# One decoder layer: four stages behind barriers replaced by one task graph ordered by a simulated list scheduler

## The chip, the cores and the metric

The kernel runs on all eight cores of one Trainium2 chip (two dies, cores 0 to 3 and 4 to 7). Each core takes one prompt sequence of 2048 rows and sixteen of the 128 sample rows, and nothing passes between cores. The metric is device microseconds of the slowest core. Names used below: TensorE (PE in the profile; PEld is its weight load), VectorE (DVE), ScalarE (ACT), GpSimd (POOL) and SyncE (SP, which here only issues DMAs).

Some executions of an eight-core program fall into a slow state, in which the cores of a die show a lower granted clock.

## The reference, cut to what matters

```python
def hybrid_layer(x, mem_k, mem_v, lru_h, lru_buf, sc_buf, ...):
    u = rmsnorm(x, norm_g)
    proj = u @ w_in                                   # (T,1024) @ (1024,8704)
    lx, lg, sb, scg, sh, sg, q, qg, mg = jnp.split(proj, SPLIT_POINTS, axis=-1)
    # branch A: conv(4) -> gated linear recurrence (width 768, 6 blocks of 128)
    xc, new_lru_buf = causal_dwconv(lx, lru_buf, lru_conv_w)
    xc = xc + lru_conv_b
    hs, new_h = rglru(xc, lru_h, ...)                 # two 128x128 gates per block, sqrt, exp, a scan over T
    z_a = (hs * jax.nn.silu(lg)) @ lru_wo
    # branch B: B * conv3(C * h)
    cy, new_sc_buf = causal_dwconv(scg * sh, sc_buf, sconv_w)
    z_b = (jax.nn.silu(sg) * sb * cy) @ sconv_wo
    # branch C: 4-head cross-attention into 256 memory tokens
    p = jax.nn.softmax(q·k / sqrt(128)); o = p·v
    z_c = (o * jax.nn.silu(qg)) @ xa_wo
    # merge, output projection, residual
    g_a, g_b, g_c = jnp.split(jax.nn.sigmoid(mg), N_BRANCH, axis=-1)
    y = (g_a * z_a + g_b * z_b + g_c * z_c) @ w_out
    return x + y, new_h, new_lru_buf, new_sc_buf      # a final rmsnorm follows outside
```

Prompt rows and sample rows share all weights. The samples have their own cached states, and their own cached keys and values (512 KB of each per sample row).

## The kernel before

It is written stage by stage: load and normalise x, keys and values; attention; branches A and B; merge; output. A barrier stands between the stages. After it, every engine listed waits until all other engines and DMAs have come as far as they had been written.

```python
    def barrier(self, skip=(), no_wait=()):
        targets = {}
        for k, st in self.streams.items():
            if st.cnt: targets[k] = st.cnt            # how far each engine has been written
        for k, v in self.dma_cnt.items():
            if v and k not in skip: targets[k] = v    # and each DMA queue
        # ... every stream not in no_wait then waits for all of them
```

The tokens are projected in two halves of 1024 (matmuls of 512 columns) and the samples apart, in matmuls of 16 columns:

```python
        HALVES = [(0, 1024), (1024, 2048)]
        def unit_half(lhs_list, rhs_arr, lo, reads):
            pp, tk = next_pp()                        # one of three PSUM tiles
            for b in range(2):
                pairs = [(lhs_list[k], rhs_arr[:, k, lo + b * 512: lo + (b + 1) * 512]) for k in range(nk)]
                mm_group(pp[:, b * 512:(b + 1) * 512], pairs, reads, tk, last_inc=(b == 1))
        def unit_samp(lhs_list, rhs_arr, reads):
            pairs = [(lhs_list[k], rhs_arr[:, k, T:TT]) for k in range(nk)]   # 16 columns
```

The order within a stage is written by hand, by stepping through generators (`adv("A", n)`, `adv("B", n - 1)`, ...).

The softmax here doesn't subtract the row's maximum and nothing guards it: scores larger than these inputs give would overflow.

## Time and profile before

| kernel before | value | where from |
|---|---|---|
| median time | 919.21 us (914.86 to 923.75, 3 runs) | the runs |
| core spans in the profiled run | 907.5 to 922.5 us | head of the page |
| TensorE busy | 782.2 us | busy table |
| next busiest engine | VectorE 427.6 us | busy table |
| 100 to 548 us (attention and branches) | TensorE busy 388 of 448 us | windows |

The prediction below quotes the lines. A busy share on the page is an average over stages: the merge stage is solid TensorE, the stages before and after are full of waits. So the windows say more than the busy table.

### The profile page before, as it was taken

The numbers are of one execution on the slowest core, as the hardware profiler recorded it, in microseconds if no ns is written. First come the engines' busy times: TensorE is split into PE (matmuls) and PEld (weight loads), VectorE is DVE, ScalarE is ACT, GpSimd is POOL, SyncE is SP. The second block draws the span as 40 slices with busy tenths as digits, with TensorE's granted clock in tenths as the row PEclk, the third lists the DMA queues.
The fourth block names the chain that finished last, engine by engine and source line by source line (L and its number), as shares of the span: only waits on it lengthen the run. The fifth ranks groups of instructions, "written<-read, shape, count | busy, mean of one in ns | idle before, by whom it ended". The sixth has DMA issues, their size and how long they took to land.

```text
span 922.5 us, 11753 instructions; the slowest of 8 cores (907.5 to 922.5 us)
## 1 busy us (share of the span) xinstructions
PE 782.2 (85%) x4199; PEld 360.4 (39%) x4199; DVE 427.6 (46%) x418; ACT 341.9 (37%) x423; POOL 238.6 (26%) x234
## 2 busy tenths in 40 slices
PE   0537799567999998999989659999999999999882
PEld 0434333123444444444444224444444444444331
DVE  0247322743244868585859692323223323323555
ACT  2414333655255564747382622111111111112332
POOL 2010056531120201112121214425435433222110
PEclk9967888678889999999999959999999999999996
DMA  8994156257470242524262307426336243003775
GB/s 174 212 223 76 47 118 158 91 77 106 42 68 1 25 45 24 46 23 47 24 58 23 35 8 69 43 26 69 30 40 69 23 47 36 12 1 97 247 239 175
DMA packets 107364, 68.58 MB, mean 74 GB/s; under 512 B 82595, under 2 KB 94965, under 8 KB 107291
## 3 DMA queue, kind: packets, MB, share of 16 engines
q0 software_dynamic: 96896, 39.26, 35.3%
q1 hardware_dynamic: 10411, 28.57, 9.7%
q8 instruction: 34, 0.56, 0.3%
q14 instruction: 23, 0.19, 0.1%
HBM read 88.96 MB, written 9.82 MB: 107 GB/s over the span
## 4 chain that ended last, share of the span: by engine, by line
PE 65%; DVE 10%; ACT 10%; DMA 8%; issue 5%; SPq 1%; POOL 0%; DVEq 0%; ACTq 0%; POOLq 0%
PE PP L365 61%; DMA R<-xp 8%; ACT R L978 2%; DVE R L962 2%; DVE R L999 1%; DVE R L1250 1%; PE PS L365 1%; ACT R L1259 1%; SPq L127 1%; DVE R L769 1%; ACT R L1056 1%; ACT R L767 1%; ACT R L768 1%; ACT R L986 1%; DVE og L771 1%
## 5 line engine op out<-in xcount | busy, mean ns | idle before, releaser
L365 PE MATMUL PP<-uT,wslot 128*128 128x512 bf16 x2176 | 511.3, 392 | 12.2 <-ACT R L1041 6.7
L365 PEld LDWEIGHTS PP<-uT,wslot 128*128 128x128 bf16 x2176 | 212.8, 100 | 277.8 <-issue 74.1
L365 PE MATMUL PP<-R 128*128 128x512 bf16 (+1 forms) x384 | 97.9, 396 | 37.3 <-DVE R L769 11.9
L1182 ACT ACTIVATE R<-PP 128x1024 f32<-128x1024 f32 x48 | 49.2, 1026 | 211.5 <-PE PP L365 206.2
L1191 DVE SCALAR_TENSOR_TENSOR R<-R,PP 128x1024 f32<-128x1024 f32 x32 | 39.1, 1221 | 152.0 <-PE PP L365 152.0
L127 POOL DMA_DIRECT2D wslot<-w_in x64 | 56.6, 904 | 52.0 <-PE PP L365 48.3
L365 PEld LDWEIGHTS PP<-R 128*128 128x128 bf16 (+1 forms) x384 | 33.6, 98 | 89.3 <-issue 57.8
L1195 POOL TENSOR_TENSOR R<-R 128x1024 f32<-128x1024 f32 x16 | 37.5, 2343 | 110.5 <-DVE R L1191 110.5
L1198 POOL TENSOR_TENSOR R<-R 128x1024 bf16<-128x1024 f32 x16 | 37.5, 2347 | 60.2 <-DVE R L1191 30.1
L810 POOL TENSOR_TENSOR R<-R 128x1024 f32<-128x1024 f32 x16 | 37.5, 2346 | 38.3 <-ACT R L809 25.0
L813 DVE TENSOR_REDUCE R<-R 128x8 f32<-128x1024 f32 x16 | 19.5, 1217 | 53.6 <-POOL R L810 53.6
L962 DVE SCALAR_TENSOR_TENSOR R<-R,pT 128x2048 f32<-128x2048 f32 x18 | 42.3, 2351 | 4.0 <-ACT R L958 2.4
L365 PE MATMUL PP<-gB,wslot 128*128 128x512 bf16 x192 | 44.1, 379 | 0.0
L365 PE MATMUL PP<-gA,wslot 128*128 128x512 bf16 x192 | 44.1, 379 | 0.0
L1187 DVE SCALAR_TENSOR_TENSOR R<-R,PP 128x1024 f32<-128x1024 f32 x16 | 19.5, 1221 | 52.4 <-PE PP L365 49.3
L1061 DVE SCALAR_TENSOR_TENSOR R<-R,pT 128x2048 f32<-128x2048 f32 x12 | 28.2, 2352 | 20.4 <-ACT R L1058 19.8
L1259 ACT ACTIVATE R<-R 128x1024 f32<-128x1024 f32 (+1 forms) x17 | 18.0, 1057 | 53.0 <-DVE stat L1274 41.1
L1250 DVE SCALAR_TENSOR_TENSOR R<-PP,R 128x1024 f32<-128x1024 f32 (+1 forms) x17 | 20.8, 1224 | 30.9 <-DMA R<-xp 21.3
L968 POOL COPY SO<-R 128x3 f32<-128x3 f32 x6 | 1.1, 187 | 129.8 <-DVE R L950 129.8
L994 DVE SCALAR_TENSOR_TENSOR R<-R 128x2064 f32<-128x2064 f32 x6 | 13.8, 2308 | 38.3 <-ACT R L993 38.3
L476 ACT ACTIVATE R<-R 128x1024 bf16<-128x1024 f32 (+1 forms) x19 | 20.1, 1058 | 29.4 <-DMA R<-xp 28.2
L365 PE MATMUL PP<-og,wslot 128*128 128x512 bf16 x128 | 30.2, 379 | 0.0
(177 smaller groups left out, 813.8 us busy)
## 6 DMA issues: line engine op xcount, KB each, us to landing
wslot<-w_in POOLq DMA_DIRECT2D x60, 256.0 KB, 8.0
R<-xp SPq DMA_DIRECT2D x16, 512.0 KB, 12.5
R<-ck SPq DMA_DIRECT2D x16, 512.0 KB, 3.6
R<-xp POOLq DMA_DIRECT2D x16, 512.0 KB, 5.6
y_p<-R SPq DMA_DIRECT2D x16, 512.0 KB, 3.1
R<-cv POOLq DMA_DIRECT2D x16, 256.0 KB, 5.3
wslot<-w_in POOLq DMA_DIRECT2D x4, 512.0 KB, 23.2
R<-w_out POOLq DMA_DIRECT2D x8, 256.0 KB, 11.5
```

The source lines that it names most:

```text
L127: eng.dma_start(out=out, in_=in_, **kw).then_inc(sems[semkey], 16)
L365: S.op("pe", lambda e, l=l, r=r, i=i: e.matmul(out_ap, l, r, start=(i == 0), stop=(i == n - 1)), reads=reads, writes=[wtok], inc=(last_inc ...
L476: S.op("act", lambda e, xb_=xb_, nr=nr, ti=ti: e.activation(out=junk[0:nr, :], in_=xb_[0:nr, :], func=AF.Square, accum_out=stat[0:nr, ti:t ...
L810: S.op("pool", lambda e, kb_=kb_, qb_=qb_: e.tensor_tensor(out=prod, in0=kb_, in1=qb_.unsqueeze(1).to_broadcast([128, 2, 512]), op=ALU.mul ...
L962: S.op("dve", lambda e, k=k, cw=cw: e.scalar_tensor_tensor(out=xc[:, 0:T], in0=lxp[:, k:k + T], scalar=cw(k), in1=xc[:, 0:T], op0=ALU.mult ...
L1061: S.op("dve", lambda e, k=k, sw=sw: e.scalar_tensor_tensor(out=cy[:, 0:T], in0=cinp[:, k:k + T], scalar=sw(k), in1=cy[:, 0:T], op0=ALU.mul ...
L1182: S.op("act", lambda e, pp=pp, th_=th_: e.activation(out=th_, in_=pp[:], func=AF.Tanh, scale=0.5), reads=[tk], writes=[tth])
L1191: S.op("dve", lambda e, th_=th_, zp=zp: e.scalar_tensor_tensor(out=th_, in0=th_, scalar=1.0, in1=zp, op0=ALU.add, op1=ALU.mult), reads=[tt ...
L1195: S.op("pool", lambda e, acc=acc, th_=th_: e.tensor_tensor(out=acc, in0=acc, in1=th_, op=ALU.add), reads=[tth, tacc_], writes=[tacc_])
L1198: S.op("pool", lambda e, acc=acc, th_=th_, j=j, lo=lo, hi=hi: e.tensor_tensor(out=mT[:, j, lo:hi], in0=acc, in1=th_, op=ALU.add), reads=[t ...
L1250: S.op("dve", lambda e, pp=pp, yr_=yr_, xr_=xr_, nr=nr: e.scalar_tensor_tensor(out=yr_[0:nr, :], in0=pp[0:nr, :], scalar=0.5, in1=xr_[0:nr ...
L1259: S.op("act", lambda e, xr_=xr_, yr_=yr_, nr=nr, col=col: e.activation(out=xr_[0:nr, :], in_=yr_[0:nr, :], func=AF.Square, accum_out=stat2 ...
```

## The change

Its intent is that nothing waits for a stage any more. Every operation becomes a task with an engine, an estimated duration, the tokens that it reads and writes (a token is the name under which a piece of data is ordered), and a priority. A list scheduler simulates the five instruction streams while the program is built. Each time, it takes a ready task of the best priority, allots ring buffers, and emits the instruction at the end of that engine's stream. The chip then runs each stream in exactly that order. 2048 + 16 rows are cut into three units of 688 with the samples inside, and the four query blocks come first, while x is still arriving. The sample products move from GpSimd to VectorE, x in the output stage gets ten buffers, and PSUM is four tiles for all.

```diff
+BLK = 344
+UW = 2 * BLK
+NU = 3
...
-        HALVES = [(0, 1024), (1024, 2048)]
...
+        def unit(lhs, nk, rhs, u, reads, prio, hold=()):
+            ps = Handle(PS)                                   # one of four PSUM tiles
+            def mm(k, b):
+                c = u * UW + b * BLK
+                return lambda e: e.matmul(ps.ap[:, b * 512:b * 512 + BLK], lhs(k), rhs[:, k, c:c + BLK], ...)
+            G.pe([mm(k, b) for k in range(nk) for b in range(2)], nk * 2 * 0.1465, reads, [ps.tok], prio, hold)
...
-        S.barrier(no_wait=("pe",))            # and the other barriers between stages
...
+    def dve(self, fn, n, reads, writes, prio, mode=1):
+        return self._add("dve", (n / mode + 170) / 960.0, [fn], reads, writes, prio)   # the planned duration
...
+                for r, t in lst:
+                    if r <= m + 0.4:                          # ready within 0.4 us of the earliest
+                        k = t.prio
+                        if t.tset is not None and curset is not None and not (t.tset & curset):
+                            k += 20.0                         # would need another ScalarE table
+                        if bk is None or k < bk[0]:
+                            bk = (k, r, t)
...
+        for hd in range(4):
+            step(heads_q, hd)                                 # queries first
+        step(branch_A_lg, 0)
+        step(branch_B_sg, 0)
+        step(branch_A_lx, 0)
+        kv(pos)
...
+        m_xr += [Mem(f"xr{4 + i}", m_gB.off + i * 4096, 1024, F32) for i in range(6)]
...
+            G.dma("sp", [(dst, lambda y_=y_, nr=nr: y_.ap[0:nr, :])], nr * 4096, [y_.tok], [t_dram[4]], P, None)
```

The scan is entered with its 2048 columns, so it is planned as (2048 + 170)/960 = 2.31 us. The last line, the store of a result tile, names one token, `t_dram[4]`, as written by all seventeen stores.

## The prediction

> **What bounds the kernel now.** I read the page's busy table first, then the slices, then a table of stretches for the slowest core, then the chain that ended last, and last some single groups. Busy time first:
>
> ```profile
> PE 782.2 (85%) x4199; PEld 360.4 (39%) x4199; DVE 427.6 (46%) x418; ACT 341.9 (37%) x423; POOL 238.6 (26%) x234
> ```
>
> TensorE is busy 85%, nothing else is above half. So the kernel is TensorE plus the times when TensorE waits or is slow. Where these lie the slices tell:
>
> ```profile
> PE   0537799567999998999989659999999999999882
> PEclk9967888678889999999999959999999999999996
> ```
>
> The barriers stand at about 100, 233, 548 and 836 us (the lines of the chain change there). Busy time of each engine between them (the last fields are granted clock, DMA share, GB/s):
>
> ```profile
> 0.00:100.00 100.00, 46.19 (x349) 32.40 (x349) 39.32 (x61) 35.94 (x71) 10.22 (x21) 0.84 0.78 158
> 100.00:233.00 133.00, 104.42 (x468) 41.04 (x468) 51.49 (x59) 59.23 (x84) 54.08 (x38) 0.77 0.53 103
> 233.00:548.00 315.00, 283.85 (x1510) 127.59 (x1511) 209.62 (x172) 168.24 (x158) 53.34 (x79) 0.94 0.36 34
> 548.00:836.00 288.00, 288.00 (x1607) 134.36 (x1605) 81.21 (x77) 52.69 (x58) 109.97 (x79) 0.99 0.36 38
> 836.00:922.50 86.50, 59.72 (x268) 24.99 (x266) 45.92 (x52) 25.81 (x52) 10.97 (x18) 0.92 0.60 202
> ```
>
> TensorE idles 53.8 us in the front (load and normalise x), 28.6 in attention, 31.1 in branches A and B, nothing in the merge stage, 26.8 in the output stage: 140 us in all. The merge stage is TensorE's own bound and shows its rate, one step of it in the chain being
>
> ```profile
> 586.29 34.55 PE PP L365 x160
> ```
>
> so a 512-column matmul costs 34.55/160 = 215.9 ns; the next step starts 35.54 us later, and the 0.99 us between them holds 40 matmuls of 16 sample columns, 25 ns each. In the last stage the chain is a load of x behind two buffers, one such pair every 9 us for two tiles:
>
> ```profile
> by line: DMA R<-xp 50.8%; DVE R L1250 12.8%; ACT R L1259 12.1%; issue 6.5%; DMA R<-xs 3.9%; ACT stat L1266 2.5%; DVE R L1217 2.4%; DVE R L1276 1.5%; ACTq L105 0.5%; DVEq L105 0.4%; DVE stat L1274 0.2%; POOLq L166 0.2%; POOLq L126 0.0%
> ```
>
> How much of the 782 busy us is slowness? Work at full rate: 512-column matmuls 2176 (projections) + 512 (merge outputs) + 96 (attention) + 48 (gates) + 272 (output) + 16 (sample queries) = 3120 x 0.2159 = 673.6; 128 of 256 columns, by half of that, 14; 608 of 16 columns x 0.025 = 15; transposes 19 x 0.9 = 17; the rest about 8. Sum **728 us**. So 922.5 = 728 of work + 140 idle + 54 of slow clock and start-up in the busy time.
>
> **What the Trainium skill says.** (1) "TensorE: Matmul & The Clock Gate", section on 56 against 53.3 ns: back-to-back warm matmuls start every N / 2.4 GHz + about 2.5 ns, never under about 25 ns. The trace agrees: 215.9 ns for 512, 25 ns for 16. So I use 344/2.4 + 2.5 = 145.8 ns for the new width, an estimate by that page.
> (2) Same page, "What's actually happening": the clock is halved after idle windows, and a peak-current limiter takes a die to 13/16 once three of its cores run dense matmuls. The trace agrees only in part: this core is at 0.81 from 113 to 270 us, and at 0.50 from 55 to 75, but the other cores mostly run at 1.00 from 200 us on, and the 288 us of fully dense merge stage are at 0.99 to 1.00 on all eight.
> (3) "SBUF — State Buffer", on the shared port pair: VectorE operations with two SBUF inputs and GpSimd lock each other out for a whole instruction. The trace agrees:
>
> ```profile
> L771 DVE TENSOR_TENSOR og<-R,og x16: 692/693/2345, 172.3 to 231.4; 128x512 bf16<-128x512 f32 x16
> ```
>
> Minimum and median are 0.69 us, the longest 2.35, which is GpSimd's sample product (2.346 us each) in the way.
>
> **The change part by part.**
> *Units of 688.* T + 16 rows = 2064 = 3 x 688, each two matmuls of 344. Matmuls of 344: 68 column blocks x 8 x 6 = 3264, gates 72, merge outputs 8 x 16 x 6 = 768: 4104 x 0.1458 = 598.4 us. Of 512: keys/values 32, attention 96, sample queries 16, output 272: 416 x 0.2159 = 89.8. Transposes 17, small ones (sample values as single columns, states) 7. Sum **712 us**, 16 less than before: six times 145.8 is 875 ns for a weight block against 4 x 215.9 + 25 = 889. The program has 4859 matmuls instead of 4199, so more weight loads, but one takes 98 ns and lies beside a matmul of 146.
> It also removes the small evacuations of samples on ScalarE and VectorE, off the path.
> *Front.* The loads of x and the weights saturate the DMA engines until 78 us now (share 1.0 and above from 25 to 75), and the first projections begin at 76.6. In the new order, a unit of 688 needs six tiles of x, about 22 us in, and the seven first blocks (queries, one A and one B block) hold 7 x 7.0 = 49 us of TensorE work with nothing but x and their weights. The two x and weight streams are still one bandwidth: 19 x-tiles of about 1.6 us (4 KB packets, some 0.17-0.2 us each over 16 engines) and twelve weight blocks of 1024 packets at 47 ns over 16 engines (that is what the merge stage shows: share 0.365 of 200 us, 24869 packets), 3.0 us each: 30 + 36, from 8 us on, so x is complete at 65 to 75 us. But it is now hidden under the queries. Idle: 22 us before the sixth tile, some hiccups after, less about 6 of transposes: **25 us**, instead of 54.
> *Attention, branches and samples without barriers.* TensorE: 37 remaining blocks x 7.0 = 259, gates 10.5, attention 21, keys/values 8, samples 7: about 305 us, against the 448 us from 100 to 548 now. Does another engine hold it? VectorE in that stretch, by the durations of the page: per branch block 5 convolution steps x 2.35, the scan 4.42, five full passes (three of 2.31, two gate products 2.30) about 11.5, the minimum 1.23, six PSUM units x 0.9 = 5.4, small 1: about 33, x 6 = 198; attention 32 x 0.69 = 22; sample products and sums, moved here from GpSimd, 16 x (1.24 + 1.22) = 39: **262 us**. ScalarE: about 33 per block with table loads of 1.28, plus 12 per head: 246. All below 305, but from the first sample product to the merge stage (128 us of VectorE by the order of its instructions) TensorE has only about 800 matmuls, 117 us, + 7. So VectorE is level or just ahead there, and I allow **18 us** of TensorE idle for the whole stretch, against 60.
> *Merge.* 8 x (40 x 6 x 0.1458 = 35.0) = 280, against 8 x 35.54. Evacuation stays far below it (VectorE 9 x 0.9 = 8 a step).
> *Output.* Ten x buffers instead of two, loads begun while the merge stage ends, and no barrier. TensorE needs 272 x 0.2159 = 58.7; 17 MB at the about 320 GB/s that the front touches are 53. So TensorE sets it, with a tail of the last tile (sum 1.2, square 1.25, root 0.7, scale 1.3, store 3): **8 us**, where 86.5 us stood for the stage.
> *Clock.* TensorE is now the bound everywhere, so slow stretches count in full: **10 us**, less than the 54 because the cold front and the gaps shrink, more than nothing because of the limiter.
> Sum: 712 + 25 + 18 + 8 + 10 = **773 us**.
>
> **The rivals.** (a) *VectorE becomes the bound between front and merge.* For: 262 of 305 us, the sample work moved onto it, and a graph whose order is fixed when it is built: if the real scan (4.42 us) is longer than planned, everything behind waits. Against: 86% still leaves room, and 22 us of PSUM reads have four buffers. It would cost 20 to 30 us more: 800. (b) *The limiter.* For: 0.81 during 157 us on two cores now; the slowest core counts. A stretch like this costs 157 x 0.19 = 30 us when TensorE is the bound: 790 to 800. Against: the dense merge stage runs at full clock. (c) *DMA in the front hides nothing*: if x is complete only at 80 us and the key and value weights, which take x's buffers, 15 us later, TensorE runs dry once: +15 us. (d) *It goes better*: the order fills the sample region too, 712 + 20 + 6 + 8 + 4 = 750.
>
> **Range and chances.** None of (a) to (c) takes back the 140 us; all three together give about 840, still 8% faster. So the sign is nearly sure; wrong only if the fixed order deadlocks into long waits on the chip. I say 773, 8 in 10 between 745 and 810; faster by over 2% 0.97, within 2% 0.02, slower 0.01.
>
> **What would show it right or wrong.** Right: TensorE busy some 92% or more of the span; slices at 9 from about the fourth on; the 344-column matmuls 146 ns apart in the merge stage; no idle gap over 5 us between 100 us and the output stage; the output stage near 60 us with TensorE in the chain instead of the x load; VectorE near 85% busy in the branches. Wrong: a VectorE line behind most of TensorE's waits before the merge stage (a), granted clock under 0.93 on most cores (b), TensorE idle behind weight or x loads between 40 and 100 us (c), or matmuls of 344 columns clearly over 146 ns apart because weight loads don't hide.

## More of the kernel before

The output stage has two x buffers, and it writes the sum of the next tile ahead of the scaling of this one:

```python
        S.barrier(no_wait=("pe",))
        xr = [carve(i * 4096, 1024, F32) for i in range(2)]
        ...
        for ti in range(len(ftiles)):
            if ti + 1 < len(ftiles):
                f_stageA(ti + 1)      # load x, 16 matmuls, y = 0.5*PSUM + x (VectorE)
            f_stageB1(ti)             # root of the mean square
            if ti + 1 < len(ftiles):
                f_stageA2(ti + 1)     # sum of squares (ScalarE)
            f_stageB(ti)              # y = y * r * g (VectorE), store
```

## The result, and the profile after

The four runs of the changed kernel took 860.31, 859.96, 882.14 and 966.19 us. The last two are slow (in the 966 us run the cores of die 0 were granted 0.80 to 0.83, in the other cores 4 and 5 had 0.93), so the fast time is 860.1. The kernel before took 918.0 beside it (914.86 to 923.75). The ratio of the two is **0.938** (95%: 0.933 to 0.943), so the kernel is faster, but by some 58 us instead of the 146 forecast, and outside the range of 745 to 810. Ratios here are the mean time of one kernel's fast runs over that of the other's in the same rounds, so they are not quite the ratio of the medians quoted.

Compare with the prediction's lines, of the page after (core 3, a fast run). First busy us and share by engine, then the slices for TensorE and its clock:

```profile
PE 742.9 (87%) x4859; PEld 460.8 (54%) x4859; DVE 386.3 (45%) x367; ACT 339.1 (40%) x398; POOL 251.2 (29%) x301
...
PE   0699989789888977979896699999999999999880
...
PEclk9999999889989989989998899999999999999996
```

TensorE starts at once, in the second slice, but between slices 8 and 23 it sits at 6 to 9 where solid nines were forecast, and the last slices look as they did before. The same in windows (window, its length, busy us of PE, PEld, DVE, ACT and POOL, granted clock, DMA share, GB/s), cut where the keys and values, the merge stage and the output stage begin:

```profile
0.00:100.00 100.00, 69.95 (x537) 48.11 (x538) 27.20 (x45) 39.01 (x63) 54.95 (x85) 0.98 0.91 159
100.00:487.00 387.00, 329.67 (x2104) 196.62 (x2102) 244.47 (x207) 225.82 (x229) 67.24 (x87) 0.93 0.45 63
487.00:771.00 284.00, 283.33 (x1955) 190.15 (x1952) 73.09 (x81) 54.73 (x72) 111.60 (x95) 1.00 0.36 39
771.00:858.40 87.40, 59.99 (x272) 25.87 (x272) 41.58 (x35) 19.53 (x34) 17.43 (x36) 0.91 0.57 197
```

Two windows are wrong: the second (387 us; the 305 us of work plus 18 had been forecast) and the last (87 us for 60 of TensorE). The merge stage is as forecast; in the chain of waits it is one piece:

```profile
523.00 247.35 PE PP L726 x1696
```

247.35/1696 = 145.84 ns for a matmul of 344 columns; the prediction had 145.8.

**A measure used below.** A busy TensorE may still be slow, so for each run the matmuls between the first key/value matmul and the first output matmul were added up at what they would take back to back, N/2400 + 0.0025 us each and never under 0.025; for 344 columns that is the rate of the merge stage. Their sum is 582.4 us (575.6 in run 4, and 589.6 in run 6, which does one query block less before that stretch). The rest of the stretch is called **lost**. It has two parts: time in which TensorE is idle, and busy time beyond that rate, which includes slow clock and whatever the rule prices too low. On cores 0, 3 and 5 the changed kernel lost 85, 88 and 87 us, 55, 58 and 57 of them idle, nearly all before 487 us. (The expectations below were written with a count that took the matmuls at the edges of its 30 us windows twice. It made the losses some 6 us too small: their 80 is 87 here, their 83 between 100 and 487 us is 86.)

Core 3, with each term of the prediction's sum:

| term | forecast | measured | how |
|---|---|---|---|
| TensorE work | 712 | 702 | at the rate above: 60.7 before the stretch, 582.4 in it, 58.7 after |
| idle in the front | 25 | 30 | up to the first key/value matmul at 101.3 |
| idle from there to the first output matmul | 18 | 58 | 670.0 less 611.7 busy |
| idle in the output stage | 8 | 27 | 87.1 less 60.0 busy |
| busy beyond the rate (slow clock) | 10 | 41 | 10.5 front, 29.3 middle, 1.3 output |
| sum | 773 | 858 | span 858.4 |

So 40 of the 85 missing us are idle time between the front and the output stage, 19 idle time of the output stage, 5 that of the front, and 31 busy time beyond the rate; the work is 10 less.

The kernel before, counted in the same way, has 720 us of work; core 1, the slowest, which was granted 0.81 for much of the time from 111 to 271 us, has 140 idle and 62 of busy time beyond the rate, and core 3, which was not, 146 and 44. So on core 3 the 51 us from 909.9 to 858.4 are 18 of work, 30 of idle time and 3 of slowness. Between front and merge stage the idle time hardly changed: 60 to 64 us before (100 to 548), 58 now. Most of the idle time that was won lies in the front (54 before, 30 now).

**The middle.** What TensorE waited for between 100 and 487 us (line waiting, line that released it: us in all, times, longest):

```profile
PE PP L1003 <- DMA R<-cv: 13.7, 2, 6.9
PE PP L726 <- ACT R L790: 7.7, 14, 1.4
PE PP L726 <- DVE R L943: 6.4, 6, 4.0
PE PP L726 <- ACT R L930: 5.8, 5, 2.4
PE PP L964 <- DVE R L832: 4.8, 1, 4.8
```

L790, L943, L930 and L832 empty PSUM: gate tanh, attention product, attention exp, and the product for branch B. Of TensorE's 57 idle us in this window, ScalarE lines ended 24, VectorE lines 19 and the cached values (cv) 14. Another 29 us are busy time beyond the rate; in seven stretches of 6.8 to 10.2 us (the first at 166.0) the granted clock was 0.50, and an estimated 18 of the 29 are due to that. No engine is the bound: VectorE is busy 244 of the 387 us, ScalarE 226. The timeline shows how TensorE can wait for a VectorE that has time (start, us, engine, line, operation; in brackets the idle time before and what ended it):

```profile
327.30 1.28 ACT L801 ACT_TABLE_LOAD   x1
328.60 2.02 ACT L801 ACTIVATE R<-R 128x2064 f32<-128x2064 f32 x1
...
330.72 2.31 DVE L803 TENSOR_TENSOR R<-R 128x2064 f32<-128x2064 f32 x1 [7.11 <-ACT R L801]
...
333.13 4.42 DVE L804 TENSOR_TENSOR_SCAN R<-R 128x2048 f32<-128x2048 f32 x1
337.47 0.15 DVE L808 TENSOR_TENSOR R<-R 128x16 f32<-128x16 f32 x1
337.72 2.31 DVE L810 TENSOR_TENSOR R<-R 128x2064 bf16<-128x2064 f32 x1
...
339.95 1.65 DVE L832 TENSOR_TENSOR R<-PP,R 128x688 f32<-128x688 f32 x2
...
340.96 0.58 PE L964 MATMUL PP<-R 16*128 16x512 bf16 x1 [4.76 <-DVE R L832]
```

VectorE first stands idle for 7.11 us, because the next instruction in its stream needs a square root (L801), and that stands in ScalarE's stream behind another long pass, four evacuations of PSUM and two table loads (from 321.24 on). Then it runs a product, the scan and another product, 9.2 us in a row. Behind these stand, in the same stream, the two evacuations L832. No PSUM tile is free meanwhile, and TensorE is dry for 4.76 us. The Trainium skill, "Perfetto Trace Analysis", section "Tensor Engine Instruction (MATMUL, LD_WEIGHTS)", says "ACT/DVE/GPSIMD are strict FIFO"; this stretch agrees: a short evacuation cannot pass a long pass written ahead of it.

**The output stage.** The chain of waits there (start, us, what):

```profile
770.40 4.79 DMA R<-xp
775.29 1.24 DVE R L1138
...
781.00 15.81 DMA y_p<-R
796.92 1.24 DVE R L1138
798.29 1.16 ACT R L1141 x2
...
801.86 1.23 DVE R L1138
803.23 1.16 ACT R L1141 x2
...
806.80 1.22 DVE R L1138
```

The first store of y, issued at 781.00, took 15.81 us to land (the median store takes 2.7). The issue queue of SyncE shows what was ahead of it:

```profile
770.40 9.73 SPq L131 DMA_DIRECT2D R<-xp  x12
781.00 0.34 SPq L131 DMA_DIRECT2D y_p<-R  x1
783.27 3.78 SPq L131 DMA_DIRECT2D R<-xp  x2
796.89 0.34 SPq L131 DMA_DIRECT2D y_p<-R  x1
```

Twelve loads of x of 512 KB each, and the second store not before 796.89, because all stores write one token and each waits until the one before has landed. With four y buffers VectorE then stood still. The loads came in one burst because the x buffers lie in memory of the attention and branch products (`m_og`, `m_gB`), which the merge stage still reads: the first load was issued at 770.40, not while the merge stage ends, as the prediction has it. After that the tiles come 4.94 us apart (801.86 to 806.80), although TensorE needs 16 x 0.2159 = 3.45 for one: sum (L1138), squares (L1141), root on GpSimd and scaling run one after the other, because the fixed order of VectorE has the scaling of a tile ahead of the sum of the next one.

### The profile page after: what moved, and what is told of

Same layout as the page of the kernel before. It is cut to its first block, busy times and chain, and to the rows that moved or that the text cites. A ratio compares the mean times of both kernels' runs of the same rounds, so it can differ in the third digit from the quotient of the medians.

```text
span 858.4 us, 13185 instructions; the slowest of 8 cores (848.3 to 858.4 us)
## 1 busy us (share of the span) xinstructions
PE 742.9 (87%) x4859; PEld 460.8 (54%) x4859; DVE 386.3 (45%) x367; ACT 339.1 (40%) x398; POOL 251.2 (29%) x301
## 4 chain that ended last, share of the span: by engine, by line
PE 64%; ACT 9%; DVE 9%; issue 9%; DMA 4%; POOL 3%; ACTq 1%; DVEq 0%; POOLq 0%; SPq 0%
PE PP L726 61%; DVE R L804 2%; ACT R L1141 2%; DMA y_p<-R 2%; DVE R L1138 2%; ACT R L790 2%; DVE R L777 1%; POOL R L621 1%; DMA R<-sconv_w 1%; DVE R L803 1%; ACT R L939 1%; DMA R<-cv 1%; PE PP L866 1%; DVE R L838 1%; POOL R L633 1%
## 5 line engine op out<-in xcount | busy, mean ns | idle before, releaser
L726 PE MATMUL PP<-R 128*128 128x344 bf16 x4104 | 632.0, 315 | 34.4 <-ACT R L790 7.7
L726 PEld LDWEIGHTS PP<-R 128*128 128x128 bf16 x4104 | 402.1, 99 | 256.9 <-issue 55.4
L1101 DVE SCALAR_TENSOR_TENSOR R<-R,PP 128x688 f32<-128x688 f32 x72 | 62.7, 871 | 202.8 <-PE PP L726 202.7
L131 POOL DMA_DIRECT2D R<-w_in x68 | 60.4, 889 | 307.0 <-PE PP L726 270.3
L1095 ACT ACTIVATE R<-PP 128x688 f32<-128x688 f32 x72 | 53.6, 744 | 218.4 <-PE PP L726 218.4
L1134 PE MATMUL PP<-R 128*128 128x512 bf16 (+1 forms) x272 | 60.0, 379 | 8.4 <-DVE R L1138 7.3
L1105 POOL TENSOR_TENSOR R<-R 128x688 f32<-128x688 f32 x24 | 39.3, 1639 | 45.6 <-DVE R L1101 44.1
L1141 ACT ACTIVATE R<-R 128x1024 f32<-128x1024 f32 (+1 forms) x17 | 18.0, 1056 | 65.9 <-DVE R L1138 65.7
L1108 POOL TENSOR_TENSOR R<-R 128x688 bf16<-128x688 f32 x24 | 38.7, 1637 | 16.9 <-DVE R L1101 16.9
L777 DVE SCALAR_TENSOR_TENSOR R<-R 128x2048 f32<-128x2048 f32 x18 | 42.2, 2347 | 2.7 <-ACT R L774 1.9
L1145 DVE SCALAR_TENSOR_TENSOR R<-R 128x1024 f32<-128x1024 f32 (+1 forms) x17 | 21.8, 1283 | 28.6 <-POOL R L621 27.2
L838 DVE SCALAR_TENSOR_TENSOR R<-R 128x2048 f32<-128x2048 f32 x12 | 28.2, 2348 | 8.8 <-ACT R L835 8.4
L790 ACT ACTIVATE R<-PP,R 128x688 f32<-128x688 f32 x36 | 28.1, 833 | 6.8 <-PE PP L726 6.7
L1138 DVE SCALAR_TENSOR_TENSOR R<-PP,R 128x1024 f32<-128x1024 f32 (+1 forms) x17 | 20.5, 1218 | 14.5 <-DMA y_p<-R 6.5
```

The source lines that it names most:

```text
L131: eng.dma_start(out=out, in_=in_).then_inc(sems[semkey], 16)
L726: return lambda e: e.matmul(ps.ap[:, b * 512:b * 512 + BLK], lhs(k), rhs[:, k, c:c + BLK], start=(k == 0), stop=(k == nk - 1))
L777: G.dve(lambda e, k=k: e.scalar_tensor_tensor(out=xc[:, 0:T], in0=lxp[:, k:k + T], scalar=cw(k), in1=xc[:, 0:T], op0=ALU.mult, op1=ALU.add ...
L790: G.act(lambda e, ps=ps, dst=dst, u=u, bcol=bcol: e.activation(out=cols(dst, u), in_=pv(ps), func=AF.Tanh, scale=0.5, bias=dv[:, bcol:bcol ...
L838: G.dve(lambda e, k=k: e.scalar_tensor_tensor(out=cy[:, 0:T], in0=cinp[:, k:k + T], scalar=sw(k), in1=cy[:, 0:T], op0=ALU.mult, op1=ALU.ad ...
L1095: G.act(lambda e, ps=pg[u], th_=th_: e.activation(out=b3(th_.ap), in_=pv(ps), func=AF.Tanh, scale=0.5), UW, [pg[u].tok], [th_.tok], Px - 2 ...
```

## The experiments

**Theories.** T1: between front and merge the time is lost by the *order* in which the planner put each stream; another order of the same instructions loses much less. Rival R1: VectorE's amount of work, or the scan planned at 2.31 instead of 4.42 us, is the cause (rival (a) of the prediction). Rival R2: the lost time belongs to work that no order can hide. T2: the output stage loses its time to the shared token of the stores. Rival R3: to VectorE's serial order alone.

**1. A token of its own for each store.**

```diff
-            G.dma("sp", [(dst, ...)], nr * 4096, [y_.tok], [t_dram[4]], P, None)
+            G.dma("sp", [(dst, ...)], nr * 4096, [y_.tok], [Tok(f"y{ti}")], P, None)
```

> Every store of y gets its own ordering token instead of one that all 17 share; nothing else changes in the source, and the plan changes only in the output stage. Theory A (the shared token makes each store wait until the one before has landed, the first of them landed 15.8 us after its issue behind twelve loads of x, and the plan built a serial order of VectorE around it): the output stage falls from 88 us to 62-70, the whole from 860 to 835-842, the ratio to the kernel before to about 0.915. Rival B (the output stage is held by DMA bandwidth, 17 MB): it stays above 80 us and the time within 5 us of 860.

Measured: 845.92 us (844.25 to 847.72), ratio 0.920 (0.916 to 0.923); still correct. The lost time of the middle stayed at 86 to 89 us, and the time is somewhat above the 835 to 842 expected. In the output stage the chain of the slowest core (core 2) is now TensorE itself:

```profile
772.92 64.35 PE PP L1134 x272
```

On core 3 the stage lasts from 770.4 to 843.5, 73 us instead of 87. The token alone accounts for some 14 us.

**2. The sum of the next tile ahead of the scaling of this one** (the order that the kernel before had), the token left shared.

```diff
+            if ti > 0:
+                G.after(tscale, tsum)      # scaling of tile ti-1 is placed after the sum of tile ti
```

> The shared token stays; only VectorE's order in the output stage is forced: the sum of tile t+1 always before the scaling of tile t. Instructions of TensorE are the same. If the serial chain sum, square, root, scale of 4.94 us a tile is the bound after the first stall (theory A, second half), the ten tiles from 797 us on go at 3.5 to 3.8 us instead of 4.94 and the time falls by 10 to 14 us, to about 848. If the landing of the stores is the bound instead, a tile still takes 4.5 us or more and the time falls by less than 5 us.

Measured: 847.04 us (844.15 to 915.9, one of them slow), ratio 0.920 (0.916 to 0.924), lost in the middle 86 to 87. The same gain as run 1 by the other way. But the chain is another one. TensorE doesn't set the stage here; the stores do, one behind another (core 3):

```profile
779.34 15.25 DMA y_p<-R
794.65 4.93 DMA y_p<-R
799.65 2.92 DMA y_p<-R
...
827.69 2.68 DMA y_p<-R
```

So neither T2 nor R3 is right as stated: the late store and the serial order are both needed for the 87 us. The first store is as late as before, but the tiles behind it now catch up at the pace of the stores, mostly 2.6 to 3.1 us each, instead of 4.94. Either remedy is enough to gain 13 to 14 us.

**3. The scan planned with its measured length.**

```diff
-                                                 op0=ALU.mult, op1=ALU.add), T, t_thr + t_thi, [t_xcP], P)
+                                                 op0=ALU.mult, op1=ALU.add), 4073, t_thr + t_thi, [t_xcP], P)
```

4073 stands for (4073 + 170)/960 = 4.42 us in the planner; the instruction is the same.

> The list scheduler is told the scan's true length (4.4 us instead of 2.3); the instructions are the same, only the order changes. Theory W (the fixed order is bad because VectorE's longest operation was planned at half its length): idle of TensorE between 100 and 487 us falls from 83 to 60 or less and the time by 15 us or more. Theory P (the order is already that sparse in the plan itself, wrong lengths are secondary): within 6 us of 860, to either side.

Measured: 850.73 us (849.10 to 909.13, one of them slow), ratio 0.924 (0.920 to 0.928). Lost 76 to 80 us, 7 to 9 less than before, which lies between the two theories. The wrong length is a cause, but a small one, and R1 in this form doesn't carry the loss.

**4. Without the samples' attention.**

```diff
-                sample_scores(pos, 5.0)
-                sample_values(pos + 90, 1.5)
+                pass
```

> Sample scores and sample values are left out (the sample rows of y are wrong on purpose). They are 7 us of TensorE work and 39 us of VectorE. If VectorE with the sample work on it holds the stretch before the merge stage and the waits for cached values (14 us) are real, the time falls by 25 to 38 us, to about 828, and the lost TensorE time between 100 us and the merge stage from 83 to 50-60. If the sample work hid in idle time anyway, it falls by no more than its own 7 us.

Measured: 819.73 us (819.51 to 820.09), ratio 0.891 (0.888 to 0.894). Lost 54 to 56 us, 31 to 32 less, beside some 7 us less of TensorE work; idle 37 to 38. The edit takes away more than 40 us of VectorE work (346.7 instead of 386.3 in the busy table): the loads of the cached keys and values go too, and the order changes. TensorE's waits for cached values (10 to 14 us) are gone, while the idle time that VectorE lines end falls only from 19 to 16. So this run doesn't show that VectorE's load holds TensorE.

**5. Without table switches** (Silu, Sqrt and Ln replaced by Tanh). The planner no longer sees switches, so the order changes too.

```diff
-EXP = frozenset((0, 6))
-SILU = frozenset((18,))
+EXP = None
+SILU = None
...
-            G.act(lambda e: e.activation(out=a2, in_=a2, func=AF.Sqrt, ...
+            G.act(lambda e: e.activation(out=a2, in_=a2, func=AF.Tanh, ...
```

> Silu, Sqrt and Ln are replaced by Tanh, so that all ScalarE functions share one table and no table is loaded between them (32 loads of 1.28 us in the changed kernel, here one or two); the planner is told so too. Results are wrong on purpose. If ScalarE's in-order queue with its table loads is what holds TensorE in the attention stretch (waits behind the gate tanh, the exponential and the product that follows it, some 33 us of the 83 lost), lost TensorE time before the output stage falls from 80 to 58-66 and the time by 14 to 22 us, to 838-846. If only the four PSUM buffers and VectorE count, it falls by less than 6 us.

Measured: 829.21 us (827.36 to 830.56), ratio 0.903 (0.897 to 0.909). Lost 56 to 57 us, 29 to 31 less, more than any expectation. ScalarE's busy time fell by 40.6 us, from 339.1 to 298.5. The idle time that ScalarE lines end fell from 24 to 17, that of VectorE lines from 19 to 8; the waits for cached values stayed at 10. So each of runs 4 and 5 alone removes some 30 of the 87 us lost, by different waits. Whether the gains of runs 3, 4 and 5 would add up was not run.

**6. Queries not first, but each right before its attention.**

```diff
-        for hd in range(4):
-            step(heads_q, hd)
...
             if n < 4:
+                step(heads_q, n)
                 step(attend, n, d=14)
```

> Undoes one part: the four query blocks are no longer projected first, each comes just before its head's attention; all else stays. If the queries are what keeps TensorE busy while x and the key and value weights load, the front loses 10 us or more: keys and values start at 100 us with fewer blocks done before, and the time rises to 868-880. If any other block does as well (the list scheduler just takes the next projections), the time stays within 5 us of 860.

Measured: 854.26 us (852.79 to 909.26, one of them slow), ratio 0.930 (0.924 to 0.936). Keys and values begin at 91 to 97 us, with one query block less before them, and the lost time is 78 to 84. The intervals of this and the changed kernel overlap a little, so whether queries first *cost* something stays open; no gain from them is seen.

**7. A first try at a barrier before the merge stage:** every later task placed after all tasks without successors of the earlier part.

> Puts one barrier back, between branches and merge stage: no engine's merge instruction before the last of the branches' instructions (weight loads excepted). If overlap there is worth what the kernel before lost at that place, the time rises by 8 to 15 us, to 868-875, all of it as TensorE idle just before the merge stage. If the branches' tail is short, it rises by less than 4 us.

Measured: 862.08 us (860.85 to 910.24, one of them slow), ratio 0.938. This says nothing about a barrier, and the edit is to blame: `G.after` orders tasks in the planner and makes no semaphore, and the planned order was nearly that already. It serves as a repeat of the changed kernel in the group of run 8: the same ratio, lost 86 to 91.

**8. Another order of the same instructions.** Runs 1 and 3 together, and other priorities, found by trying values in the planner.

```diff
-                    if r <= m + 0.4:
+                    if r <= m + 0.3:
...
-            P = P - 4                      # the long passes of branch A
+            P = P + 10
...
-                P1 = P + tb * 3            # attention
+                P1 = P + tb * 11
...
-        PC = 7.05
+        PC = 7.5
-                branch_A_gates(n, pos + 6)
+                branch_A_gates(n, pos + 14)
-                step(attend, n, d=14)
+                step(attend, n, d=7)
-                sample_scores(pos, 5.0)
+                sample_scores(pos + 20, 2)
-        PM = pos
+        PM = pos + 20
```

> Same instructions as the changed kernel, another order: own tokens for the stores of y, the scan planned at its true length, and other priorities (the four column blocks of a head's attention spread over 33 instead of 9 units of priority, gates later, sample work later). If the lost TensorE time is a matter of the fixed order, it falls from 80 to 50-58 before the output stage, and with the 14 us of the output stage the time is 812-825. If it is set by ScalarE's and VectorE's load whatever the order, the gain is that of the tokens and the scan alone: 835 or more.

Measured: **804.42 us** (802.95 to 806.93), ratio 0.876 (0.871 to 0.881), correct, and below the 812 to 825 us expected. It beats both kernels: 12.4% less than before, and, by the two ratios, 0.876/0.938 = 0.934 of the changed kernel. Core 3 in windows:

```profile
0.00:100.00 100.00, 69.40 (x546) 48.30 (x547) 27.18 (x45) 39.00 (x63) 55.63 (x85) 1.00 0.90 156
100.00:449.00 349.00, 321.64 (x2081) 196.13 (x2080) 236.53 (x205) 237.79 (x238) 69.17 (x83) 0.94 0.51 71
449.00:736.00 287.00, 286.14 (x1964) 191.96 (x1962) 81.94 (x84) 57.24 (x75) 113.69 (x99) 1.00 0.36 39
736.00:805.40 69.40, 59.12 (x272) 26.30 (x272) 41.10 (x35) 19.54 (x34) 20.14 (x36) 0.96 0.71 247
```

The same 4859 matmuls and the same VectorE instructions (386.8 us busy) run here, and ScalarE is even busier (353.6) for eleven table loads more. Yet the cores lose 47 to 54 us instead of 85 to 88 in the middle, and the output stage takes 69.4. TensorE's idle time in the middle is halved, 28 to 29 us instead of 55 to 58. What is left of it (core 3) begins with

```profile
PE PP L726 <- ACT R L790: 12.7, 21, 3.0
PE PP L726 <- DVE R L832: 5.8, 4, 3.3
```

ScalarE lines end 21 us of it (24 before), VectorE lines 6 (19 before), cached values none (10 to 14 before). Against R1 and R2 this is the decisive run: with the same work, or a little more, TensorE idles half as long. T1 holds for that half; what is left, no order that I tried removed.

**9. A barrier with semaphores:** TensorE's merge gate projections also read every token of branches A and B and of attention.

```diff
-                pg = proj(C_MG + x * 1024 + j * 128, Px, hold=[(t,) for t in ths])
+                pg = proj(C_MG + x * 1024 + j * 128, Px, hold=[(t,) for t in ths],
+                          extra=[t for g in t_gA + t_gB for t in g] + [t for g in t_og for t in g])
```

> The barrier of e7 had no semaphore behind it (the added dependencies only order the plan), so it is put back for real: TensorE's first merge instruction reads the tokens of all gated branch and attention products, and waits for them. If the overlap there is worth what the kernel before lost at that place, TensorE idles 8 to 15 us just before the merge stage and the time rises to 868-875 (ratio about 0.95). If the branches' tail is hidden in losses that stand there anyway (the late cached values), it rises by less than 4 us.

Measured: 874.00 us (873.69 to 874.36), ratio 0.953 (0.950 to 0.955). Lost 100 to 102 us. The wait is seen where the merge stage begins (core 5):

```profile
493.22 1.44 PE L1055 MATMUL PP<-R 128*54 128x128 f32 x6 [2.38 <-POOL R L845]
501.92 18.34 PE L726 MATMUL PP<-R 128*128 128x344 bf16 x108 [7.25 <-DVE R L842]
```

So having no barrier at this one place is worth (0.953 - 0.938) x 918 = 14 us. That part of the change's intent works.

**10. The priorities of run 8 alone:** the token shared, the scan length wrong.

> Only the priorities of e8, without its own tokens for the stores and with the scan at its wrong length. If the order is what counts before the output stage, the lost TensorE time there falls from 80 to 45-55 and the time to 825-835 (ratio about 0.905); the output stage stays near 86 us. If the scan's length or the tokens carried e8, it stays above 845.

Measured: 837.53 us (837.14 to 838.70), ratio 0.913 (0.911 to 0.916). Lost 62 to 66 us, against 85 to 88: the priorities alone give 21 to 25 us, a little less than expected. TensorE's idle time is 35 to 36 us, of which VectorE lines end 10 and cached values 1 to 2. What run 8 has beyond them is the output stage (87 us on core 3 here, 69 there) and another 13 to 16 us in the middle with the right scan length; about half of that is busy time beyond the rate, and the two runs were on different chips.

| version | us | ratio to before | lost in the middle |
|---|---|---|---|
| changed kernel | 860.1 (fast) | 0.938 | 85 to 88 |
| 1 own store tokens | 845.92 | 0.920 | 86 to 89 |
| 2 sum ahead of scaling | 847.04 | 0.920 | 86 to 87 |
| 3 scan length | 850.73 | 0.924 | 76 to 80 |
| 4 no sample attention | 819.73 | 0.891 | 54 to 56 |
| 5 no table switches | 829.21 | 0.903 | 56 to 57 |
| 6 queries late | 854.26 | 0.930 | 78 to 84 |
| 9 barrier before merge | 874.00 | 0.953 | 100 to 102 |
| 10 priorities | 837.53 | 0.913 | 62 to 66 |
| 8 priorities, scan, tokens | 804.42 | 0.876 | 47 to 54 |

The versions ran in three groups on different chips; the kernel before ran in each (medians 918 to 922), so the ratios are what to compare. Where a median's range ends above 900, its slow runs are left out of the ratio; without them the medians of runs 2, 3, 6 and 7 are 846.4, 850.3, 853.8 and 861.0 us.

**What the plan itself says.** This was worked out off the chip, by building each run's kernel with `build_program(verbose=True)` and reading the planner's log; it is no measurement. The plan of the changed kernel spans 849 us (858 measured), and in it TensorE idles 59 us between the first key/value and the first output matmul (55 to 58 measured). The plans of runs 10 and 8 have 35 us there (35 to 36 and 28 to 29 measured). The planned output stage takes 101 us, and 72 with run 1's tokens (87 and 73 measured). So most of the loss stood in the plan and could have been read before the chip ran. Telling the planner the true scan length doesn't shorten its own idle time (60 us), though the chip's fell to 49 to 50.

## Why the prediction was wrong

**Right: the sign, and TensorE's work.** The 688-row units cost what was worked out: 145.84 ns for a matmul, 283 us for the merge stage where 280 was forecast, and 301 us of matmul time at the full rate between 100 and 487 us where 305 was. More weight loads stayed hidden (99 ns each).

**Right in mechanism, off in size: the front.** TensorE is busy 70 of the first 100 us instead of 46, and keys and values begin at 101.3. The forecast of 25 us idle became 30, beside 10.5 us of busy time beyond the rate. Run 6 shows no gain from queries first; x arriving in units of 688 and the free choice among blocks are left as the source, and these were not tested apart.

**Wrong: "So VectorE is level or just ahead there, and I allow 18 us of TensorE idle for the whole stretch".** This step failed: TensorE idled 55 to 58 us, about as long as before the change. The step went from sums of busy time (VectorE 262, ScalarE 246, both below 305) to a small idle time. The sums were good enough: 244 and 226 measured in the window. (The items listed for a branch block add up to 35.3 and not 33, so VectorE's sum should have read 273; it changes nothing in the argument.) The inference was not. Being below TensorE in the sum did not bound the waits here, where each stream runs in a fixed order, each waits for the others several times per block, and only four PSUM tiles lie between. Run 8 shows that half of the idle time is order. The prediction also had no term for sample values that arrive late, 10 to 14 us of the idle time.

The prediction also gave itself the wrong ground against its rival (a): "86% still leaves room, and 22 us of PSUM reads have four buffers". The rival's remark on the fixed order and the scan had the direction right, but VectorE did not become the bound (it ended 19 us of the idle time, less than ScalarE), and the scan's length alone is worth 7 to 9 us of loss in run 3. Of the prediction's signs of being right, TensorE is busy 87% and not 92%, the longest wait is 6.9 us and not under 5, and VectorE is busy 63% and not 85% between 100 and 487 us.

A missing term can be sized from the rows. The 36 gate units take TensorE two matmuls each, 2 x 0.146 = 0.29 us, and ScalarE 0.83 each to empty (L790, mean 833 ns). Where six of them run together, TensorE falls behind by 0.54 us for each, 36 x 0.54 = 19 us in all, an estimate. TensorE's idle time ended by L790 is 8.4 us in the changed kernel (core 3) and 13.0 of 28 in run 8, so run 8 did not reduce this. That gates must be spaced by projections was not tested by itself.

**Wrong: "So TensorE sets it, with a tail of the last tile ...: 8 us".** The stage took 87 us, not 67. The forecast counted TensorE's and the DMA's work and read neither the token of the stores nor the order of sum and scaling. With the token mended (run 1) TensorE sets it on the slowest core, in one chain piece of 64 us; with the order mended (run 2) the stores set it. In run 8 the stage lasts 69.4 us, 10.6 beyond its 58.7 of work, close to the 8 forecast once the obstacle is gone.

**The clock.** The profiled run shows no long stretch at 0.81; rival (b) is seen only in slow runs, which are not compared. Mean granted clock on the eight cores is 0.958 to 0.962. The slices with 8 for the clock are slices with 6 to 8 for TensorE, so part of the term may follow from the waits instead of standing beside them; that was not tested. The term was too small: 41 us of busy time lie beyond the full rate, where 10 were forecast. In the middle 29 lie there, of which an estimated 18 fall into stretches at 0.50.

**What is not settled.** How much of the 87 us lost each of ScalarE, VectorE and the cached values causes: runs 3, 4 and 5 were not combined, and all three also change the order. What of the 47 to 54 us that run 8 still loses could be had by an order I did not find is open too. And only the barrier before the merge stage was put back; the worth of the others, and of the units by themselves, was not measured apart.

## What to carry to other kernels

A busy sum below the bound engine's says at best what can be reached, not what an order fixed in advance will reach: read where short evacuations stand behind long passes in the same stream, and count what a unit takes to fill against what it takes to empty. A scheduler that plans from durations is only as good as its table and its priorities, so read the idle time of its own plan before you believe a forecast; here two constants, one token and a handful of priorities were worth as much as the whole change (860 to 804 us, against 918 to 860). Before believing in a stage that "TensorE sets", look at each wait written for its stores and at which of two dependent steps comes first in the stream.

## What the Trainium skill lacked or had wrong

- "TensorE: Matmul & The Clock Gate", section "Seeing it yourself", has the peak-current limiter hold a die at 13/16 while dense matmuls on three or more of its cores last. Eight cores run the merge stage, 284 us of dense matmuls, at a granted clock of 1.00 on each (487 to 771 us); a clock of 0.80 to 0.83 over a whole run was seen in only one of the four executions of the changed kernel. In the kernel before, from 191.5 to 271 us, cores 0 and 1 were granted 0.81 and cores 2 and 3 of the same die 0.98 and 1.00. (The prediction names the section "What's actually happening" for the limiter too; it stands in this one.)
- "ScalarE: Activation LUTs", section "What ACT_TABLE_LOAD costs", gives 1283 ns for the load and 1380 ns of drain, 2.66 us for each switch. The load is 1283 ns here too, but no gap of that kind is seen: at 327.30 a load of 1.28 us begins, 17 ns after the activation before it, and the activation behind it starts at 328.60, 0.02 us after the load ends. Taking out 31 of 32 loads took 40.6 us from ScalarE's busy time, 1.3 us each.
- No page that I read gives the time that a store waits behind loads issued before it. Here a 512 KB store behind twelve loads of the same queue landed after 15.81 us, against 2.7 in the median.
